# Low weight parts subtracted half a piece later, and the attention's side work in one queue

## The chip, the cores and the metric

The kernel runs on one core of a Trainium2 chip. The metric is the device time of one execution in microseconds (us). The kernel before took 1976.13 us in the median of 3 runs (1970.66 to 1978.91). Engines are called as in the profile: PE (matmul), PEld (its weight loads), DVE (VectorE), ACT (ScalarE), POOL (GpSimd), SP (the queue that issues the DMAs).

## What is computed

Two decoder layers on x (1024 tokens, 1024 features) with a memory of 256 tokens, in float32, and a final RMS norm. Layer 1 runs an RG-LRU, a dilated attention and a memory attention side by side. Layer 2 is native sparse attention (16 heads in 2 groups; compressed, selected and window branch) and a memory attention. Both add a projected, SiLU-gated result to x. The part of layer 2 around which the change moves work:

```
k_cmp = compress_tokens(kc, pe_k, phik_w1, phik_w2)
v_cmp = compress_tokens(vc, pe_v, phiv_w1, phiv_w2)
o_cmp, p_cmp = compressed_attention(q, k_cmp, v_cmp, slopes)
o_slc = selected_attention(q, ks, vs, p_cmp, slopes)
o_win, _ = banded_attention(q, kw, vw, slopes, WIN_SIZE - 1, 1)
o = gates[..., 0:1] * o_cmp + gates[..., 1:2] * o_slc + gates[..., 2:3] * o_win
...
return x + (y.astype(x.dtype) @ w_out)
```

## The kernel before

**Weights.** All projections multiply a weight matrix in pieces of 128 columns by up to eight 128-row blocks. Each piece comes by one DMA into a tile `raw` (line 201). POOL rounds it to a short float, `wh` (line 215; for the very first pieces DVE rounds a part), and DVE subtracts, `wl = raw - wh` (line 216). A product is then three matmuls: high weight by high input, high by low, low by high. `w()` (line 187) hands out piece i and at that moment asks for the load of piece i+2 and for both parts of piece i+1. `raw`, `wh` and `wl` share a ring of six buffers, so the rounding of piece i+1 must wait until PE is done with piece i-1.

**Order.** The program is written as Python generators that are advanced step by step; the steps' order is the order in which instructions are written. A scheduler then places them on each engine by what it takes to be ready, and each engine works its own list strictly in order. So an instruction at the head of a list that waits holds everything behind it.

**The start.** Eight rows of x (`xraw`, index k) arrive one by one. ACT makes the high part `xh` (line 296), DVE the low part `xl` (line 297), and PE multiplies each by the first two pieces at once. POOL adds the squares (`ssum`, line 323). At k = 6 the third and fourth piece are prefetched, and a manual dependency keeps what DVE does of that behind that k's `xl` (lines 939 to 945).

**The attention of layer 2.** `nsa_attention` (line 1609) runs 128 works: 16 iterations `it` of (half of the tokens, head group, query block), each with 8 works of two heads. A work has scores (`nsa_scores`: PE line 1507 into banks `s` or `big`, DVE line 1516 for mask and maximum into `P`, ACT line 1518 for the exponential, DVE line 1521 and POOL line 1524 to scale `P`) and their use (`nsa_apply`: PE transposes, line 1537; ACT and DVE split the result into `ph` and `pl`, lines 1541 and 1542; `nsa_av` multiplies by the values, line 1563, and ends in `ot`, line 1570). Scores run some works ahead. Between them stand two fillers: `fill` (projections of the second half of the tokens, line 239 with output `f`, drained by DVE in `st`, line 1786 or 1767; later the output projection, line 1130) and `side`.

**Side work.** `side_steps(it)` prepares what comes next: the query operands of iteration it+1 (`nsa_query`, mostly POOL), the compressed branch of iteration it+2 (`nsa_cmp`), and at some iterations the keys of the next segment (`nsa_group`). Each half of a work takes one step, in iterations 2, 6 and 11 two; what is left at the end of an iteration is run at once. `nsa_cmp` is a chain: PE scores (line 1400), DVE subtract and maximum (1403, 1406), POOL subtract (1408), ACT exponential (1410), DVE sum and reciprocal (1412, 1413), DVE gate factors `cmx` (1433), POOL multiply `ce` (1434; in the second half 1418 and 1431), then `CMPW` extra pauses, then PE transposes (1441), which ACT and DVE copy to `pc` (1442, 1443). The first matmul of an output tile (line 1558) reads `pc`.

Of the kernel before, what the change touches and what calls it, by code (L numbers as in the profile page):

```python
# [13 lines left out]
ALU = mybir.AluOpType  # L14
# [26 lines left out]
LOOK = (3, 3, 2, 3)  # L41
DELAY = 3
FILL0, FILL1 = (4, 3, 2.2, 1.8), (3.2,)
CMPW = 2


def f32(ap):
    return ap.bitcast(F32)


class Trunk:
    def __init__(self, ctx, tc, a):
        self.ctx, self.tc, self.nc, self.a = ctx, tc, tc.nc, a
        self.uid = 0
        self.rings = {}
        nc = tc.nc
        self.const = ctx.enter_context(tc.tile_pool(name="const", bufs=1))
        self.U = ctx.enter_context(tc.tile_pool(name="U", bufs=NU))
        self.W = ctx.enter_context(tc.tile_pool(name="W", bufs=NW))
        self.H = ctx.enter_context(tc.tile_pool(name="H", bufs=NH))  # L60
        self.sm = ctx.enter_context(tc.tile_pool(name="sm", bufs=2))
        self.ps = ctx.enter_context(tc.tile_pool(name="ps", bufs=1, space=PSUM))
        self.wide = None
        self.psum_layout(True)
        ctx.callback(lambda: self.bs.close())
        self.dr = ctx.enter_context(tc.tile_pool(name="dr", bufs=1, space=DRAM))
        self.ident = self.const.tile([128, 128], F32, name="ident")
        make_identity(nc, self.ident)
        self.vec = self.const.tile([128, V_N], F32, name="vec")
        nc.sync.dma_start(self.vec, a["vec"])  # L70
        self.ones = self.const.tile([128, 2], F32, name="ones")
        nc.vector.memset(self.ones, 1.0)
        self.memrow, self.memops, self.xt = None, {}, []
        self.plan, self.raws, self.split_w = [], [], []
        self.pos = 0
        self.side = []
        self.back, self.ticks = None, 0
        self.chained = None
# [105 lines left out]
    def pieces(self, *srcs, tile=None):  # L184
        self.plan += [(src, tile or self.wt) for src in srcs]

    def w(self):

        i = self.pos
        self.pos += 1  # L190
        self.prefetch(i + 3, i + 2)
        r = self.split_w[i]
        self.split_w[i] = None
        return r

    def prefetch(self, n_raw, n_split):
        nc = self.nc
        for j in range(len(self.raws), min(n_raw, len(self.plan))):
            src = self.plan[j][0]
            raw = self.wt("raw", F32, src.shape)  # L200
            nc.sync.dma_start(raw, src)
            self.raws.append(raw)
        for j in range(len(self.split_w), min(n_split, len(self.plan))):
            raw = self.raws[j]
            tile = self.plan[j][1]
            kn, c = raw.shape[1:]
            if kn * c <= 512:
                t = tile("wp", F32R, (128, 2, kn, c))
                h, l = t[:, 0], t[:, 1]
            else:  # L210
                h = tile("wh", F32R, raw.shape)
                l = tile("wl", F32R, raw.shape)
            for k0, k1 in ((0, 1), (1, kn)) if j < 2 else ((0, kn),):
                e = nc.vector if j < 2 and k0 == 0 else nc.gpsimd
                e.tensor_scalar(h[:, k0:k1], raw[:, k0:k1], 1.0, 0.0, op0=ALU.mult, op1=ALU.add)  # L215
                nc.vector.tensor_tensor(l[:, k0:k1], raw[:, k0:k1], f32(h[:, k0:k1]), op=ALU.subtract)  # L216
            self.split_w.append((h, l))
            self.raws[j] = None

    def round_to(self, h, src):  # L220
        self.nc.gpsimd.tensor_scalar(h, src, 1.0, 0.0, op0=ALU.mult, op1=ALU.add)

    def proj(self, x, halves=(0, 1)):

        w = self.w()
        ps = self.big()
        for k in range(8):
            self.proj_step(ps, w, x, k, halves)
            if x[k][0][0].shape[-1] == 512 or k % 4 == 3:
                self.tick()  # L230
        return ps

    def proj_step(self, ps, w, x, k, halves=(0, 1)):
        h, l = w
        for i, (w, p) in enumerate(((h, 0), (h, 1), (l, 0))):
            for j, t in enumerate(halves):
                v = x[k][t][p]
                o = ps[j] if isinstance(ps, list) else ps[:, 512 * j:512 * j + v.shape[-1]]
                self.nc.tensor.matmul(o, w[:, k, :], v,  # L239
                                      start=(k == 0 and i == 0), stop=(k == 7 and i == 2))  # L240
# [842 lines left out]
    def out_half(self, res):  # L1083

        nc = self.nc
        ssum = self.u("ssum", F32, (128, 512))
        for c in range(8):
            if c % 2 == 0:
                pair = self.u("x3", F32, (128, 2, 512))
            r = pair[:, c % 2, :]  # L1090
            nc.sync.dma_start(r, res[128 * c:128 * c + 128, 0:512])
            ps = self.fbank()
            for j, k in enumerate(NSA_K):
                y = self.split_pair(0, k // 2)
                if j % 4 == 0:
                    w = self.w()
                self.out_step(ps, w, y, j, slice(0, 512))
                yield
            nc.vector.tensor_tensor(r, ps, r, op=ALU.add)
            self.add_square(r, c, ssum)  # L1100
            if c % 2:
                nc.sync.dma_start(self.x3d[c - 1:c + 1].rearrange("c p n -> p c n"), pair)
            yield
# [22 lines left out]
    def out_step(self, ps, w, y, j, cols):  # L1126
        h, l = w
        yh, yl = y
        for i, (ww, v) in enumerate(((h, yh), (h, yl), (l, yh))):
            self.nc.tensor.matmul(ps[:, cols], ww[:, j % 4, :], v[:, NSA_K[j] % 2, cols],  # L1130
                                  start=(j == 0 and i == 0), stop=(j == 9 and i == 2), skip_group_check=True)
# [260 lines left out]
    def nsa_cmp(self, it):  # L1392

        nc = self.nc
# [37 lines left out]
        else:  # L1432
            nc.vector.tensor_tensor(mx[:, 3], mx[:, 2], gt[:, 0], op=ALU.mult)
            nc.gpsimd.tensor_tensor(e, e, mx[:, 3, :, None].to_broadcast([128, 8, 64]), op=ALU.mult)
        for _ in range(1 + CMPW):
            yield
        pcs = self.u("pc", F32R, (128, 2, 512))
        for quad in range(2):
# [170 lines left out]
    def nsa_attention(self, fill0, fill1):  # L1609
# [33 lines left out]
        while nxt < LOOK[0]:  # L1643
            run(self.nsa_scores(works[nxt]))
            nxt += 1
        side = iter(())
        fill, due, rate = fill0, 0.0, FILL0
        for i, W in enumerate(works):
            it = i // 8
            if i == 126:  # L1650
                self.split_pair(1, 2)
            if i % 8 == 0:
                run(side)
                side = side_steps(it)
            if i == 64:
                run(fill)
                for p in range(2):
# [2 lines left out]
            new = []  # L1660
            while nxt < min(i + LOOK[it // 4] + 1, len(works)):
                while works[nxt]["key"][0] not in self.AB:
                    next(side)
                new.append(self.nsa_scores(works[nxt]))
                nxt += 1
            ap = self.nsa_apply(W)
            n = (self.key_range(W)[1] + 1) // 2
            for h in range(2):
# [3 lines left out]
                run(fill, int(due))  # L1672
                due -= int(due)
                run(ap, (n * (h + 1)) // 2 - (n * h) // 2)
                run(side, 2 if it in (2, 6, 11) else 1)
            for sc in new:
                run(sc)
            run(ap)
# [94 lines left out]
    def fill_proj(self, x, row):  # L1773

        nc = self.nc
        for c in list(range(8)) + [16, 17] + list(range(8, 16)):
            w = self.w()
            ps = self.fbank()
            for k in range(8):
                self.proj_step(ps, w, x, k, (1,))  # L1780
# [189 lines left out]
```

## Time and profile before

| | |
|---|---|
| median of 3 runs | 1976.13 us |
| the profiled execution, its own time | 1968.65 us |
| its span from first to last instruction | 1966.9 us |
| PE busy | 1882.4 us, 96% of the span |
| DVE busy | 1181.5 us, 60% |
| ACT busy | 839.8 us, 43% |
| POOL busy | 826.0 us, 42% |
| matmuls | 10018 |
| mean granted clock of PE | 0.991 of full speed |

The profile says which engine did what and when, and for an engine that sat idle what ended the idle time. PE is nearly always busy, so only its idle stretches, and the stretches in which its clock is at half, can be won or added to. A row of the order of time begins with start and length in us, and ends with the idle time just ahead of it in brackets.

### The profile page before, as it was taken

What the parts mean: (1) busy time and instruction counts of PE and PEld (TensorE: products, weight loads), DVE (VectorE), ACT (ScalarE), POOL (GpSimd) and SP (SyncE); (2) the same over time, 40 slices, a digit from 0 to 9 for tenths busy, and PEclk for the clock granted to TensorE, in tenths of its full rate; (3) what the DMA queues carried; (4) which work ended last, traced back from release to release, by engine and by line L of the source; (5) the groups of instructions that cost most, each with busy time, mean ns of one, the idle gap of its engine ahead of it and who ended that gap; (6) DMA issues with size and microseconds to landing.
All of it is one profiled execution on the core that took longest, in us unless ns stands there. A gap on an engine that the chain in (4) does not pass through costs nothing. (4 is left out here: it accounts for less than half of the span.)

```text
span 1966.9 us, 27378 instructions
## 1 busy us (share of the span) xinstructions
PE 1882.4 (96%) x10018; PEld 1590.3 (81%) x10018; DVE 1181.5 (60%) x2293; ACT 839.8 (43%) x1780; POOL 826.0 (42%) x941
## 2 busy tenths in 40 slices
PE   8999999999999999999999999999998999988997
PEld 6789988887877777888888878787777887877886
DVE  6544336535344856562143574678688877889864
ACT  4210024423212623330034351467558666788851
POOL 6231102122124434422224433577676555567533
PEclk9999999999999999999999999999999999999999
DMA  5123311113110111132222413221221112210013
GB/s 184 54 97 122 115 53 33 33 54 107 54 47 29 43 43 43 42 121 81 83 81 91 135 62 105 78 83 63 72 93 55 52 49 80 89 57 33 12 59 98
DMA packets 57286, 141.90 MB, mean 72 GB/s; under 512 B 8256, under 2 KB 16960, under 8 KB 57152
## 3 DMA queue, kind: packets, MB, share of 16 engines
q1 hardware_dynamic: 57152, 140.16, 22.2%
q8 instruction: 79, 1.29, 0.3%
q14 instruction: 55, 0.45, 0.1%
HBM read 120.21 MB, written 19.92 MB: 71 GB/s over the span
## 5 line engine op out<-in xcount | busy, mean ns | idle before, releaser
L215 POOL TENSOR_SCALAR wh<-raw 128x1024 fp32r<-128x1024 f32 (+2 forms) x149 | 169.5, 1139 | 642.1 <-PE big L239 271.6
L216 DVE TENSOR_TENSOR wl<-raw,wh 128x1024 fp32r<-128x1024 f32 (+4 forms) x151 | 194.5, 1292 | 180.7 <-POOL wh L215 158.9
L1524 POOL TENSOR_SCALAR P<-P,nden,gates 128x640 f32<-128x640 f32 (+7 forms) x256 | 214.0, 846 | 133.7 <-DVE nden L1521 112.1
L239 PE MATMUL big<-xh,wh 128*128 128x512 f32 x752 | 258.3, 423 | 1.6 <-ACT xh L296 1.1
L239 PE MATMUL big<-xl,wh 128*128 128x512 f32 x752 | 243.2, 399 | 2.8 <-DVE xl L297 2.8
L239 PE MATMUL big<-xh,wl 128*128 128x512 f32 x752 | 235.1, 393 | 0.0
L1518 ACT ACTIVATE P<-P,nden 128x640 f32<-128x640 f32 (+7 forms) x256 | 187.6, 733 | 89.6 <-DVE nden L1516 83.9
L1542 DVE TENSOR_TENSOR pl<-t,ph 128x512 fp32r<-128x512 f32 (+1 forms) x304 | 183.3, 615 | 36.1 <-ACT ph L1541 30.8
L1541 ACT ACTIVATE ph<-t 128x512 fp32r<-128x512 f32 (+1 forms) x304 | 159.6, 534 | 57.0 <-PE t L1537 46.7
L1537 PE MATMUL t<-ident,P 128*128 128x128 f32 x1056 | 167.3, 277 | 16.8 <-DVE pl L1542 13.6
L239 PEld LDWEIGHTS big<-xl,wh 128*128 128x128 f32 x752 | 141.4, 189 | 33.6 <-DVE xl L297 3.8
L1537 PEld LDWEIGHTS t<-ident,P 128*128 128x128 f32 x1056 | 126.0, 141 | 50.7 <-DVE pl L1542 12.2
L239 PEld LDWEIGHTS big<-xh,wl 128*128 128x128 f32 x752 | 141.9, 189 | 30.1
L239 PEld LDWEIGHTS big<-xh,wh 128*128 128x128 f32 x752 | 135.2, 190 | 37.3 <-issue 15.5
L239 PE MATMUL big<-x,wh 128*128 128x512 f32 x480 | 144.3, 395 | 0.0
L1563 PE MATMUL acc<-ph,nv 128*128 128x256 f32 x528 | 128.1, 310 | 6.2 <-ACT ph L1541 5.6
L1563 PE MATMUL acc<-pl,nv 128*128 128x256 f32 x528 | 121.8, 298 | 0.0
L1516 DVE CUSTOM_DVE_ANT_0 P<-big,mask 128x640 f32<-128x640 f32 (+3 forms) x128 | 116.7, 914 | 3.6 <-PE big L1507 2.0
L239 PEld LDWEIGHTS big<-x,wh 128*128 128x128 f32 x480 | 87.8, 188 | 16.4
L1563 PEld LDWEIGHTS acc<-ph,nv 128*128 128x128 f32 x528 | 86.3, 190 | 14.1 <-ACT ph L1541 11.7
L519 DVE SCALAR_TENSOR_TENSOR df<-big,row 128x1024 f32<-128x1024 f32 x23 | 39.9, 1737 | 92.8 <-PE big L239 88.1
L239 PE MATMUL f<-x,wh 128*128 128x512 f32 x288 | 93.5, 402 | 0.0
(341 smaller groups left out, 4189.3 us busy)
## 6 DMA issues: line engine op xcount, KB each, us to landing
raw<-nw_f SPq DMA_DIRECT2D x42, 512.0 KB, 3.5
raw<-hw_dv SPq DMA_DIRECT2D x24, 512.0 KB, 3.5
raw<-hw_dil SPq DMA_DIRECT2D x22, 512.0 KB, 3.5
raw<-now SPq DMA_DIRECT2D x32, 256.0 KB, 2.6
raw<-hw_z SPq DMA_DIRECT2D x14, 512.0 KB, 3.5
raw<-how SPq DMA_DIRECT2D x16, 448.0 KB, 3.4
raw<-hw_xa SPq DMA_DIRECT2D x8, 512.0 KB, 3.5
res<-xT SPq DMA_DIRECT2D x8, 512.0 KB, 5.0
```

The lines of the kernel that those rows point to most:

```text
L215: e.tensor_scalar(h[:, k0:k1], raw[:, k0:k1], 1.0, 0.0, op0=ALU.mult, op1=ALU.add)
L216: nc.vector.tensor_tensor(l[:, k0:k1], raw[:, k0:k1], f32(h[:, k0:k1]), op=ALU.subtract)
L239: self.nc.tensor.matmul(o, w[:, k, :], v, start=(k == 0 and i == 0), stop=(k == 7 and i == 2))
L519: self.nc.vector.scalar_tensor_tensor(ot[:, sl], p.rearrange("p (i r) -> p i r", r=dil), sc, rt[:, sl], op0=ALU.mult, op1=ALU.mult)
L1516: nc.vector.tensor_tensor_reduce(ev, sv, mv, scale=1.0, scalar=3e38, op0=ALU.add, op1=ALU.min, accum_out=den[:, 0, h:h + 1])
L1518: nc.scalar.activation(e, e, AF.Exp, bias=den[:, 0, h:h + 1], scale=-1.0, accum_out=den[:, 1, h:h + 1])
L1524: nc.gpsimd.tensor_scalar(es[h], es[h], den[:, 2, h:h + 1], gt[:, 2 - br, hh:hh + 1], op0=ALU.mult, op1=ALU.mult)
L1537: nc.tensor.transpose(t[:, 256 * i + 128 * h:256 * i + 128 * h + 128], W["e"][h][:, 128 * k:128 * k + 128], self.ident)
L1541: nc.scalar.activation(ph[:, :w], t[:, :w], AF.Copy)
L1542: nc.vector.tensor_tensor(pl[:, :w], t[:, :w], f32(ph[:, :w]), op=ALU.subtract)
L1563: nc.tensor.matmul(o, V[:, k0 + k, :], x[:, 256 * i:256 * i + 256], start=False, stop=(br == 1 and k == nb - 1 and x is pl), skip_group_ch ...
```

## The change

The low part of a piece is no longer written right behind the rounding. It goes on a list, `lows`, which `weight_low()` empties: at the latest at the next `w()`, in projections and the output projection in the middle of the current piece, elsewhere at once as before. For the first two pieces nothing changes. The side generators go into one queue, which is advanced at a rate that a table `SIDE` gives for each iteration; nothing is run at once at an iteration's end, and what a work needs (`AB`, `pc`) is forced just ahead of it. The compressed branch of the first half waits four pauses, not two, before its transposes.

```
-CMPW = 2
+CMPW = (4, 2)
+SIDE = (1, 1, 1.6, 1.1, 1, 1, 1.6, 1.1, 1, 1, 1, 1.7, 1.1, 1.2, 1, 1)
...
-    def w(self):
+    def w(self, later=False):
         i = self.pos
         self.pos += 1
+        self.weight_low()
         self.prefetch(i + 3, i + 2)
+        if not later:
+            self.weight_low()
...
                 e.tensor_scalar(h[:, k0:k1], raw[:, k0:k1], 1.0, 0.0, op0=ALU.mult, op1=ALU.add)
-                nc.vector.tensor_tensor(l[:, k0:k1], raw[:, k0:k1], f32(h[:, k0:k1]), op=ALU.subtract)
+                self.lows.append((l[:, k0:k1], raw[:, k0:k1], f32(h[:, k0:k1])))
+                if j < 2:
+                    self.weight_low()
...
+    def weight_low(self):
+        while self.lows:
+            l, raw, h = self.lows.pop(0)
+            self.nc.vector.tensor_tensor(l, raw, h, op=ALU.subtract)
...
     def proj_step(self, ps, w, x, k, halves=(0, 1)):
         h, l = w
+        if k == 4:
+            self.weight_low()
...
     def out_step(self, ps, w, y, j, cols):
         h, l = w
         yh, yl = y
+        if j % 4 == 2 or j == 9:
+            self.weight_low()
...
-        for _ in range(1 + CMPW):
+        for _ in range(1 + CMPW[half]):
             yield
...
             if i % 8 == 0:
-                run(side)
-                side = side_steps(it)
+                sides.append(side_steps(it))
...
                 while works[nxt]["key"][0] not in self.AB:
-                    next(side)
+                    step()
...
+            while it not in self.pc:
+                step()
             ap = self.nsa_apply(W)
...
-                run(side, 2 if it in (2, 6, 11) else 1)
+                lag += SIDE[it]
+                for _ in range(int(lag)):
+                    step()
+                lag -= int(lag)
```

`proj`, `fill_proj` and `out_half` call `w(True)`.

DVE at the start, from the low part of the second x row on; before:

```order
L297 SCALAR_TENSOR_TENSOR xl_143<-xraw_91,vec,xh_142 128x1024
L216 TENSOR_TENSOR wl_116<-raw_93,wh_115 128x896
L297 SCALAR_TENSOR_TENSOR xl_167<-xraw_127,vec,xh_166 128x1024
L297 SCALAR_TENSOR_TENSOR xl_191<-xraw_146,vec,xh_190 128x1024
L297 SCALAR_TENSOR_TENSOR xl_215<-xraw_170,vec,xh_214 128x1024
L297 SCALAR_TENSOR_TENSOR xl_239<-xraw_194,vec,xh_238 128x1024
L297 SCALAR_TENSOR_TENSOR xl_263<-xraw_218,vec,xh_262 128x1024
L216 TENSOR_TENSOR wl_271<-raw_266,wh_270 128x1024
L297 SCALAR_TENSOR_TENSOR xl_293<-xraw_242,vec,xh_292 128x1024
```

The same place in the changed kernel (its lines 311 and 230 are 297 and 216 before):

```order
L311 SCALAR_TENSOR_TENSOR xl_143<-xraw_91,vec,xh_142 128x1024
L230 TENSOR_TENSOR wl_116<-raw_93,wh_115 128x896
L311 SCALAR_TENSOR_TENSOR xl_167<-xraw_127,vec,xh_166 128x1024
L230 TENSOR_TENSOR wl_271<-raw_266,wh_270 128x1024
L311 SCALAR_TENSOR_TENSOR xl_191<-xraw_146,vec,xh_190 128x1024
L311 SCALAR_TENSOR_TENSOR xl_215<-xraw_170,vec,xh_214 128x1024
L311 SCALAR_TENSOR_TENSOR xl_239<-xraw_194,vec,xh_238 128x1024
L311 SCALAR_TENSOR_TENSOR xl_263<-xraw_218,vec,xh_262 128x1024
L311 SCALAR_TENSOR_TENSOR xl_292<-xraw_242,vec,xh_291 128x1024
```

The low part of the third piece is written outside the stretch that the manual dependency covers and moves ahead of four `xl`. Nothing moves on POOL and ACT there. On SP the load of the last x row falls behind the load `raw_316`, which waits for a buffer that this low part frees; the changed kernel:

```order
L932 DMA xraw_194<-xT 128x1024
L932 DMA xraw_218<-xT 128x1024
L205 DMA raw_316<-hw_dil 128x1024
L932 DMA xraw_242<-xT 128x1024
L205 DMA raw_413<-hw_dil 128x1024
```

Before, `xraw_242` stands right behind `xraw_218`.

DVE in iteration 3 of the attention, from the compressed branch's sum (`cmx<-ce`) to its gate factors (`cmx<-cmx,gates`); before:

```order
L1412 TENSOR_REDUCE cmx_10453<-ce_10451 128x8
L1516 ISA P_10505,nden_10504<-s_10537,mask_7914 128x512
L1516 ISA nden_10504 128x1
L1771 SCALAR_TENSOR_TENSOR st_10511<-th_10513,st_10511 128x512
L1542 TENSOR_TENSOR pl_10526<-t_10520,ph_10525 128x512
L1413 RECIPROCAL cmx_10453<-cmx_10453 128x8
L216 TENSOR_TENSOR wl_10545<-raw_10271,wh_10544 128x1024
L1433 TENSOR_TENSOR cmx_10453<-cmx_10453,gates 128x8
```

The same in the changed kernel (1428, 1449 and 1532 are 1412, 1433 and 1516 before):

```order
L1428 TENSOR_REDUCE cmx_10432<-ce_10430 128x8
L1558 TENSOR_TENSOR pl_10494<-t_10488,ph_10493 128x512
L1429 RECIPROCAL cmx_10432<-cmx_10432 128x8
L1537 RECIPROCAL nden_10459<-nden_10459 128x2
L1532 ISA P_10509,nden_10508<-s_10510,mask_7914 128x512
L1532 ISA nden_10508 128x1
L1449 TENSOR_TENSOR cmx_10432<-cmx_10432,gates 128x8
L1794 SCALAR_TENSOR_TENSOR st_10515<-f_10276,row_7051 128x512
L1532 ISA P_10509,nden_10508<-s_10537,mask_7914 128x512
L1532 ISA nden_10508 128x1
L230 TENSOR_TENSOR wl_10545<-raw_10271,wh_10544 128x1024
```

The gate factors go ahead of the low part, and less stands between them and the sum; iteration 2 shows the same. On PE the transposes that read `ce` move behind the first four value matmuls of iteration 4.

DVE at the first low part that is subtracted behind scores of the attention; before:

```order
L1542 TENSOR_TENSOR pl_9209<-t_9205,ph_9208 128x256
L1516 ISA P_9217,nden_9216<-s_9218,mask_7914 128x128
L1516 ISA nden_9216 128x1
L1786 SCALAR_TENSOR_TENSOR st_9223<-f_9146,row_7051 128x512
L216 TENSOR_TENSOR wl_9229<-raw_9140,wh_9228 128x1024
L1516 ISA P_9217,nden_9216<-s_9237,mask_7914 128x128
L1516 ISA nden_9216 128x1
```

The same in the changed kernel (its 1558, 1532 and 1813 are 1542, 1516 and 1786 before):

```order
L1558 TENSOR_TENSOR pl_9209<-t_9205,ph_9208 128x256
L1532 ISA P_9217,nden_9216<-s_9218,mask_7914 128x128
L1532 ISA nden_9216 128x1
L1813 SCALAR_TENSOR_TENSOR st_9223<-f_9145,row_7051 128x512
L1532 ISA P_9217,nden_9216<-s_9236,mask_7914 128x128
L1532 ISA nden_9216 128x1
L230 TENSOR_TENSOR wl_9229<-raw_9140,wh_9228 128x1024
```

One score tile of `P` goes ahead of the low part. At the other low parts of the first half the place moves by none to two such tiles; POOL's list there, with the query operands ahead of `wh`, stays nearly as it was. From iteration 8 to 10 no engine's list changes, and in layer 1 only a few places do.

## Rows read from the trace of the kernel before

**Rows 1.** Stretches of the span: length, busy us (count) of PE, PEld, DVE, ACT, POOL; clock, DMA share, GB/s.
```profile
0.00:50.00 50.00, 44.13 (x184) 35.09 (x185) 31.84 (x49) 22.86 (x32) 31.66 (x27) 0.93 0.51 181
...
600.00:1050.00 450.00, 449.53 (x1966) 361.73 (x1965) 227.45 (x184) 147.25 (x167) 140.50 (x83) 1.00 0.20 65
...
1240.00:1510.00 270.00, 247.23 (x1476) 207.38 (x1474) 208.93 (x564) 168.04 (x439) 187.12 (x228) 0.99 0.24 77
1510.00:1700.00 190.00, 175.85 (x1112) 152.52 (x1112) 155.38 (x333) 125.82 (x247) 108.51 (x119) 0.98 0.19 58
1700.00:1900.00 200.00, 185.18 (x1304) 164.72 (x1303) 176.59 (x388) 166.10 (x332) 122.79 (x125) 0.99 0.11 37
```

**Rows 2.** PE, clock, DMA share, GB/s: a half-clock stretch, one at full, another at half.
```profile
15.30:18.70 3.40, 3.40 (x10) 0.50 1.04 406
...
1399.00:1409.00 10.00, 7.28 (x39) 1.00 0.29 80
1431.90:1435.30 3.40, 3.40 (x12) 0.51 0.55 217
```

**Rows 3.** Low parts that DVE waited for, and PE behind them, in order of time.
```profile
1265.80 1.23 DVE L216 TENSOR_TENSOR wl<-raw,wh 128x1024 fp32r<-128x1024 f32 x1 [3.20 <-POOL wh L215]
...
1267.29 0.33 PE L1507 MATMUL s<-K,A 128*128 128x128 f32 x1 [1.13 <-DVE nden L1516]
...
1398.33 1.23 DVE L216 TENSOR_TENSOR wl<-raw,wh 128x1024 fp32r<-128x1024 f32 x1 [3.74 <-POOL wh L215]
...
1402.02 0.47 PE L1558 MATMUL acc<-pc,vc 128*128 128x512 f32 x1 [2.39 <-DVE ot L1570]
...
1431.29 0.39 PE L1507 MATMUL s<-K,A 128*128 128x256 f32 x1 [1.80 <-DVE nden L1516]
```

**Rows 4.** Waits of PE, 1240 to 1510 us: what waited, for whom; us, times, longest.
```profile
PE s L1507 <- DVE nden L1516: 7.4, 10, 1.8
PE t L1441 <- POOL ce L1434: 4.0, 2, 2.1
PE acc L1558 <- DVE ot L1570: 3.6, 4, 2.4
...
PE t L1441 <- POOL ce L1431: 1.3, 1, 1.3
```

**Rows 5.** Waits of DVE, 1240 to 1510 us.
```profile
DVE wl L216 <- POOL wh L215: 17.4, 11, 3.7
```

**Rows 6.** The start in order of time: DVE, POOL, PE, SP.
```profile
16.62 11.00 DVE L297 SCALAR_TENSOR_TENSOR xl<-xraw,vec,xh 128x1024 fp32r<-128x1024 f32 x5
27.55 2.31 DVE L216 TENSOR_TENSOR wl<-raw,wh 128x1024 fp32r<-128x1024 f32 x1
...
20.06 2.02 POOL L215 TENSOR_SCALAR wh<-raw 128x1024 fp32r<-128x1024 f32 x1
...
39.39 1.06 POOL L215 TENSOR_SCALAR wh<-raw 128x1024 fp32r<-128x1024 f32 x1
...
14.66 0.74 PE L239 MATMUL big<-xl,wh 128*128 128x512 f32 x2 [2.30 <-DVE xl L297]
...
21.86 0.61 PE L239 MATMUL big<-xl,wh 128*128 128x512 f32 x2
...
11.28 1.61 SPq L918 DMA_DIRECT2D xraw<-xT  x2
29.89 0.33 SPq L201 DMA_DIRECT2D raw<-hw_dil  x1
```

**Rows 7.** Groups of PE's matmuls, 21 to 40 us, by shape: busy us, mean ns, idle.
```profile
L239 PE MATMUL big<-xl,wh 128*128 128x512 f32 x21 | 6.5, 389 | 0.0
```

**Rows 8.** Waits of PE, 0 to 50 us.
```profile
PE t L245 <- POOL ssum L323: 0.5, 2, 0.4
```

**Rows 9.** The two waits for `ce` in order of time: PE, DVE, POOL.
```profile
1333.77 0.63 PE L1441 MATMUL t<-ident,ce 128*64 128x128 f32 x4 [1.94 <-POOL ce L1434]
1375.33 0.63 PE L1441 MATMUL t<-ident,ce 128*64 128x128 f32 x4 [2.06 <-POOL ce L1434]
...
1372.24 1.83 DVE L216 TENSOR_TENSOR wl<-raw,wh 128x1024 fp32r<-128x1024 f32 x1
1374.00 0.15 DVE L1433 TENSOR_TENSOR cmx<-cmx,gates 128x8 f32<-128x8 f32 x1
...
1374.23 1.04 POOL L1434 TENSOR_TENSOR ce<-ce,cmx 128x512 f32<-128x512 f32 x1 [1.24 <-DVE cmx L1433]
```

More of the change, by code (lines that the diff above doesn't have):

```diff
@@ L73, in __init__ @@
         self.memrow, self.memops, self.xt = None, {}, []
-        self.plan, self.raws, self.split_w = [], [], []
+        self.plan, self.raws, self.split_w, self.lows = [], [], [], []
         self.pos = 0
@@ L223, in proj @@
     def proj(self, x, halves=(0, 1)):
-        w = self.w()
+        w = self.w(True)
         ps = self.big()
@@ L1095, in out_half @@
                 if j % 4 == 0:
-                    w = self.w()
+                    w = self.w(True)
                 self.out_step(ps, w, y, j, slice(0, 512))
@@ L1645, in nsa_attention, with step @@
             nxt += 1
-        side = iter(())
+        sides, lag = [], 0.0
+        def step():
+            while sides:
+                try:
+                    return next(sides[0])
+                except StopIteration:
+                    sides.pop(0)
         fill, due, rate = fill0, 0.0, FILL0
@@ L1776, in fill_proj @@
         for c in list(range(8)) + [16, 17] + list(range(8, 16)):
-            w = self.w()
+            w = self.w(True)
             ps = self.fbank()
```

## The prediction

> **What bounds the kernel now.** I read the stretches first. PE is busy 449.53 of 450 us between 600 and 1050, and about 92% of the attention: 247.23 of 270, 175.85 of 190 and 185.18 of 200 us [rows 1]. So PE sets the time nearly everywhere. What can be won is its idle time, which is 5.9 us in the first 50 and 22.8, 14.2 and 14.8 us in the three stretches of the attention, and the stretches in which its clock is at half. The layer-1 projections hold little. The clock is read next: matmuls run at 1.2 instead of 2.4 GHz in a stretch of 3.40 us at the start and of 3.40 at 1432, while after a wait of 2.39 us at 1399.6 it stays at 1.00 [rows 2, 3]. Such a stretch of 3.4 us loses half of it, 1.7.
>
> Then I read the waits. In 1240 to 1510, where the change moves most, PE waits 7.4 us for DVE before scores, 4.0 in two waits for `ce`, 3.6 for DVE's `ot`, 1.3 for another `ce` [rows 4]. DVE itself waits 17.4 us in 11 low parts for POOL's rounding [rows 5]; that is what the change is about. What counts is how much of these 17.4 us PE feels. The low parts in order of time say: the one at 1265.80 had waited 3.20 us, and PE behind it 1.13; the one at 1398.33 had waited 3.74, and PE 2.39; PE's wait of 1.80 at 1431.29 has another such low part ahead of it [rows 3]. Outside the attention PE does not feel it: between 600 and 1050 it is idle for 0.47 us in all [rows 1]. Low parts that come later there are worth nothing and, since the list is emptied in the middle of the piece, half a piece ahead of their first reader, cost nothing either. If that cover were gone, each piece would cost at most its low part, 1.23 us.
>
> **The start: a cost.** The changed order puts the low part of the third piece ahead of four `xl`. The five `xl` run from 16.62, 11.00 us together, 2.2 each, so the first ends at 18.8 [rows 6]. The low part now stands next, and must wait for POOL's rounding, which ran 20.06 to 22.08. Its 2.02 us beside DVE's work compare with 1.06 for the same operation at 39.39 [rows 6]; with DVE waiting it ends between 21.1 and 22.1. Then the low part takes between 1.23 us, as at 1265.80 [rows 3], and 2.31, as at 27.55 [rows 6], and the `xl` of the fourth row 2.2: ready between 24.55 and 26.6. PE began that row's `xl` products at 21.86 [rows 6], so it idles 2.7 to 4.7 us. I take 3.2: the rounding at its fast end, as DVE does nothing beside it, and the low part halfway. The next rows of x are covered again, since one `xl` of 2.2 us is followed by seven matmuls of 0.389 us [rows 7], 2.7 us of PE. A wait of 2.30 us at 14.66 stood ahead of the half-clock stretch from 15.30 [rows 2, 6]; a new one of over 2.7 us there, with PE's work still broken, is likely to bring another, 1.7 us; the wait of 2.39 without a fall [rows 2, 3] bounds this at nothing. The `ssum` waits of 0.5 us [rows 8] come later than the new gap and vanish in it. Start: 3.2 + 1.7 - 0.5 = +4.4, between +2.2 and +7.6 (4.7 and two stretches of 1.7, less 0.5).
>
> The Trainium skill, "SBUF — State Buffer", section "Who interferes with whom", says that a DVE instruction with two inputs from SBUF and a GpSimd instruction that reads SBUF lock each other out. The trace agrees where it shows 2.02 beside 1.06 for one rounding and 2.31 beside 1.23 for one low part [rows 3, 6]. By that rule a waiting DVE would leave both at their fast end, and the start would come to 2.7 + 1.7 - 0.5 = +3.9 rather than +4.4.
>
> On SP the load of the last row of x falls behind `raw_316`. That load went out at 29.89, when the low part of the third piece had set its buffer free, whereas the pairs of x rows went out from 11.28 [rows 6]. In the changed kernel that low part ends some 5 to 6 us earlier, at 22.4 to 24.4, and the last row follows. From issue to use it needs its transfer, ACT's high part and an `xl`; four rows of 2.7 us and the new gap of 3.2 put that use 14 us after 21.86, so I take nothing for it. If the transfer is slow the last row costs PE up to an estimated 1.6 us, which goes into the bound.
>
> **The two waits for `ce`: a gain.** At 1375.33 PE had waited 2.06 us for `ce`. POOL had waited 1.24 for DVE's `cmx`, which stood behind a low part of 1.83 us at 1372.24 [rows 9]. In the changed order the gate factors go ahead of that low part, so `ce` comes about 1.8 us earlier, and the transposes of this iteration move behind four value matmuls: the wait goes. The wait of 1.94 at 1333.77 [rows 9] has the same build. The distance on PE between the chain's start and its transposes is about the same there, but the gate factors come earlier. Both gone: -4.0. The bounds are none, if POOL's own list is what ends last, and all. I take all, since the trace names DVE as what POOL waited for. What is late next is DVE's score work, which PE waits for in 10 places already [rows 4].
>
> **One low part behind a score tile: a gain.** At 1265.80 DVE had waited 3.20 us with a score tile queued behind the low part, and PE behind that waited 1.13 [rows 3]. One tile now goes ahead: -1.1, bounds 0 and -1.1. At the other low parts of 1240 to 1510 the rounding stays behind the same operations in POOL's list, and the low part moves by no more than two tiles. I leave the 2.39 and the 1.80 [rows 3] where they are.
>
> **The side queue.** In iteration 6 the rate falls from 2 to 1.6 per half work and the distance from `ce` to its transposes on PE becomes shorter by about 1.5 us by my estimate. There PE waited 1.3 us for `ce` of line 1431 [rows 4]. It could grow by as much, or shrink as POOL and DVE have less at once. I take 0, and 1.3 each way. Iterations 8 to 10 are unchanged. In 11 to 14 little moves; the idle 14.8 us of 1700 to 1900 [rows 1] are taken as they are, give or take 1.
>
> **Sum.** Start +4.4, `ce` -4.0, score tile -1.1: -0.7 us. The profiled execution took 1968.65 us, so 1967.95, a ratio of 0.9996. The median of the runs shown is 1976.13, 0.4% above this execution; the ratio on it gives 1975.4. A measurement of this kernel tells about 0.5% from no change, 9.9 us: faster is below 1966.2, slower above 1986.0.
>
> **Rivals.** *A: the attention loses its DVE waits.* If the later low parts and the steady pace keep DVE from standing in front of POOL at all, then the waits for `nden` (7.4) and `ot` (3.6) [rows 4] and the half-clock stretch at 1432 (1.7) [rows 2] go too: -0.7 - 12.7 = -13.4 on the profiled execution, 1962.7 on the median. For it: 17.4 us of DVE waiting [rows 5] against some 11 us of PE's waits. Against it: the low parts stay right behind the rounding's neighbours at 1398 and 1428, with POOL's list unchanged, and half of the stretch's idle time has no low part ahead.
>
> The Trainium skill, "TensorE: Matmul & The Clock Gate", section "HAM oscillation — how this bites in real kernels", says that idle gaps between groups of matmuls send the clock down, and that each such fall is paid for anew. The rows agree at 14.66 and 1431.29 and not at 1399.6, where 2.39 us of waiting left the clock at full [rows 2, 3, 6]. If each long gap counted, A would be worth more, and the start's new gap would surely cost its 1.7.
>
> *B: the low part at the head of DVE's list at the start costs its upper bound.* Rounding and low part both run at their slow ends (4.7 us of idle), two half-clock stretches follow (3.4) and the last row of x is late (1.6): +9.2 after the 0.5. Against the gains of 5.1 that is +4.1, or 1980.2; if the `ce` waits stay too, because POOL's multiply and not DVE's gate factors ends last, it is +8.1, 1984.3; with iteration 6's wait grown by 1.3 and another half-clock stretch of 1.7 behind it, +11.1, 1987.3. It is slower than before from the point at which the start costs more than 5.1 us. For it: the slow ends are what the start shows, with POOL's squares beside DVE's low part. Against it: DVE would be idle while POOL rounds.
>
> *C: the change does not do what it says.* The scheduler may put the low part right behind the rounding's end as before, since it orders by readiness; the third order above moves it by one tile only. Then the start's cost stands alone: +4.4, 1980.5.
>
> **How the numbers follow.** My forecast has 0.56. A has 0.22, as DVE waits for 17.4 us and a steadier queue may take more of this than I can follow. B has 0.14, of which about 0.08 lies above 0.5%, since its end does and the price of a broken start may be larger than the rows of before show; C has 0.08, with 0.02 above. Faster by over 0.5%: A and 0.01 of the forecast, 0.23. Slower: 0.10. Same: 0.67. The range goes from 1962, which takes in the better half of A's results, to 1987, near the end of B.
>
> **What would show it.** A wait of PE for an `xl` near 21.9 us, 3 us long, and a half-clock stretch behind it, would show the start's cost; no such wait would show it wrong. The rows `t <- ce` of line 1434 should be gone from PE's waits in 1240 to 1510. DVE's wait for `wh` there should stay above 10 us, and the waits of PE near 1400 and 1430 should stay; if `s <- nden` falls well below 5 us and `ot` vanishes, A is right. If the last row's `xl` ends a wait of PE near 36 us, B's late load is real. PE's idle time in 600 to 1050 should stay below 1 us; if it grows to several, the low parts come too late for their readers, and the forecast fails on that step.

## The result and the profile after

The changed kernel took 1984.43 us in the median of 9 runs, the kernel before 1973.92 in 9 runs beside them: a ratio of 1.0054, 95% interval 1.0043 to 1.0066. It is slower by about 10.5 us. The forecast was 1975.4 and no change that can be measured; the time lies inside the stated range, near its upper end.

The profiled execution of the changed kernel has a span of 1981.2 us, 14.3 more than the one before. The stretches, with the columns of [rows 1]:

```profile
0.00:50.00 50.00, 41.47 (x157) 32.53 (x158) 30.80 (x46) 20.38 (x28) 31.26 (x26) 0.93 0.49 178
600.00:1050.00 450.00, 449.53 (x1975) 362.00 (x1974) 225.14 (x182) 144.68 (x165) 144.60 (x92) 1.00 0.19 63
1240.00:1510.00 270.00, 245.13 (x1412) 207.50 (x1411) 199.81 (x547) 161.11 (x421) 180.19 (x220) 0.96 0.23 73
1510.00:1700.00 190.00, 174.96 (x1123) 152.45 (x1122) 156.97 (x341) 124.03 (x250) 107.78 (x121) 0.98 0.19 58
1700.00:1900.00 200.00, 183.47 (x1278) 162.39 (x1277) 175.84 (x391) 168.49 (x334) 127.18 (x129) 1.00 0.13 44
```

Against [rows 1] PE does the same 449.53 us of work in 600 to 1050, loses 2.7 us of busy time in the first 50, and in 1240 to 1510 it is busy 245.13 rather than 247.23 us at a clock of 0.96 rather than 0.99; 1412 matmuls fall into that stretch against 1476.

A busy share does not tell where the time was lost, since the same work lies at other times in the two traces. So I matched matmuls: the n-th matmul of one line and width in the one trace with the n-th of that line in the other, and took the median of the difference of their start times in each stretch. This is how far the changed kernel lags:

| time in the kernel before, us | lag, us | what lies between |
|---|---|---|
| 100 to 1100 | 4.8 to 4.9 | the start |
| 1200 to 1236 | 4.1 | |
| 1288 to 1292 | 2.4 | a gain of 1.7 |
| 1296 to 1300 | 8.9 | a loss of 6.5, of which 2.6 come back by 1308 |
| 1460 to 1464 | 7.9 | 1.6 more since 1308 |
| 1472 to 1476 | 12.9 | a loss of 5.0 |
| 1600 to 1700 | 12.0 | |
| 1830 to 1900 | 14.6 | a loss of 2.5 |

The waits of PE in 1240 to 1510 us: what waited, for whom, us in total, times, longest. They answer to [rows 4]; lines 1523, 1574, 1457, 1447 and 1450 are 1507, 1558, 1441, 1431 and 1434 before.

```profile
PE s L1523 <- DVE nden L1532: 12.5, 12, 3.6
PE acc L1574 <- DVE ot L1586: 3.8, 3, 2.4
PE t L1457 <- POOL ce L1447: 3.2, 1, 3.2
...
PE t L1457 <- POOL ce L1450: 0.2, 1, 0.2
```

The waits for `ce` of the first half (4.0 us in [rows 4]) are down to 0.2. But the waits for DVE's scores went from 7.4 to 12.5, and the wait for the other `ce` from 1.3 to 3.2. DVE's own wait for the rounding grew from 17.4 [rows 5] to 21.0 us:

```profile
DVE wl L230 <- POOL wh L219: 21.0, 11, 4.0
```

**The place near 1294 us.** The kernel before, in order of time, DVE, POOL and then PE:

```profile
1289.36 0.42 DVE L1516 CUSTOM_DVE_ANT_0 P<-s,mask 128x256 f32<-128x256 f32 x1
...
1290.90 0.41 DVE L1516 CUSTOM_DVE_ANT_0 P<-s,mask 128x256 f32<-128x256 f32 x1
...
1293.30 1.23 DVE L216 TENSOR_TENSOR wl<-raw,wh 128x1024 fp32r<-128x1024 f32 x1 [1.97 <-POOL wh L215]
...
1292.22 1.05 POOL L215 TENSOR_SCALAR wh<-raw 128x1024 fp32r<-128x1024 f32 x1
...
1291.45 0.28 PE L1507 MATMUL s<-K,A 128*128 128x256 f32 x1
```

The changed kernel, DVE, POOL and PE:

```profile
1291.52 0.17 DVE L1537 RECIPROCAL nden<-nden 128x2 f32<-128x2 f32 x1 [1.62 <-ACT P L1534]
1295.67 1.23 DVE L230 TENSOR_TENSOR wl<-raw,wh 128x1024 fp32r<-128x1024 f32 x1 [3.99 <-POOL wh L219]
...
1297.42 0.41 DVE L1532 CUSTOM_DVE_ANT_0 P<-s,mask 128x256 f32<-128x256 f32 x1
...
1291.18 1.28 POOL L1479 TENSOR_TENSOR B<-q,A 64x512 fp32r<-64x512 f32 x1
1292.54 0.62 POOL L233 TENSOR_SCALAR A<-A 64x512 fp32r<-64x512 f32 x1
1293.23 1.27 POOL L1479 TENSOR_TENSOR B<-q,A 64x512 fp32r<-64x512 f32 x1
1294.59 1.05 POOL L219 TENSOR_SCALAR wh<-raw 128x1024 fp32r<-128x1024 f32 x1
...
1297.89 0.58 PE L1523 MATMUL s<-K,A 128*128 128x256 f32 x1 [3.64 <-DVE nden L1532]
```

Before, two score tiles `P` ran on DVE while POOL worked through the query operands, and PE had its scores' bank free in time. In the changed kernel the low part stands ahead of these two tiles. DVE waits 3.99 us for `wh`, which stands behind three query operands on POOL, and PE waits 3.64 us behind it. `wh` itself is no later than before: 1294.59 against 1292.22 us, which is the lag of 2.4. Half-clock stretches stand at this wait, at one near 1439 and at one near 1479 (length, PE busy, clock, DMA share, GB/s); the first and the last begin while PE still waits:

```profile
1297.00:1303.80 6.80, 5.91 (x19) 0.50 0.33 117
1440.30:1443.70 3.40, 3.40 (x12) 0.50 0.38 149
1477.90:1484.70 6.80, 5.22 (x20) 0.50 0.13 55
```

Between 1240 and 1900 us half clock takes 27.2 us in all in this execution, 13.6 in the one before. PE is busy in 24.1 and 12.3 us of it, and half of that is lost: 5.9 us of matmul time more than before. The wait near 1439:

```profile
1438.96 0.39 PE L1523 MATMUL s<-K,A 128*128 128x256 f32 x1 [3.08 <-DVE nden L1532]
```

### The profile page after: what moved, and what is told of

Same layout as the page of the kernel before. It is cut to its first block, busy times and chain, and to the rows that moved or that the text cites. A ratio compares the mean times of both kernels' runs of the same rounds, so it can differ in the third digit from the quotient of the medians.

```text
span 1981.2 us, 27387 instructions
## 1 busy us (share of the span) xinstructions
PE 1890.0 (95%) x10018; PEld 1599.1 (81%) x10018; DVE 1179.6 (60%) x2293; ACT 841.4 (42%) x1780; POOL 825.0 (42%) x941
## 5 line engine op out<-in xcount | busy, mean ns | idle before, releaser
L1553 PEld LDWEIGHTS t<-ident,P 128*128 128x128 f32 x1056 | 127.6, 142 | 50.0 <-DVE pl L1558 10.6
L253 PEld LDWEIGHTS big<-x,wh 128*128 128x128 f32 x480 | 87.7, 188 | 16.6 <-POOL wh L219 0.4
```

Of the source, the lines that this page charges most:

```text
L253: self.nc.tensor.matmul(o, w[:, k, :], v, start=(k == 0 and i == 0), stop=(k == 7 and i == 2))
L1553: nc.tensor.transpose(t[:, 256 * i + 128 * h:256 * i + 128 * h + 128], W["e"][h][:, 128 * k:128 * k + 128], self.ident)
```

## The experiments

All ratios are against runs of the kernel before on the same chip, with 95% intervals, from 6 to 12 runs of each kernel and 9 to 24 of the one before. A difference of two ratios is known to some 0.0015, 3 us, no better.

| kernel | ratio | interval |
|---|---|---|
| changed kernel | 1.0054 | 1.0043 to 1.0066 |
| e1_start: its start put right | 1.0031 | 1.0019 to 1.0042 |
| e2_lows: before + later low parts | 1.0024 | 1.0012 to 1.0035 |
| e3_side: changed without later low parts | 1.0034 | 1.0020 to 1.0047 |
| e5_cmpw: before + four pauses | 0.9996 | 0.9987 to 1.0005 |
| e6_rate: e1_start, all old rates | 0.9994 | 0.9985 to 1.0002 |
| e10_rate6: e1_start, old rates in 6 and 7 | 1.0020 | 1.0011 to 1.0030 |
| e12_rate2: e1_start, old rates in 11 to 13 | 1.0015 | 1.0003 to 1.0026 |
| e4_act: before, ACT rounds in the attention's first half | 0.9939 | 0.9927 to 0.9951 |
| e9_dummy: the same, POOL rounds too, for nothing | 0.9990 | 0.9982 to 0.9999 |
| e8_act_cmpw: e4_act + four pauses | 0.9936 | 0.9923 to 0.9948 |
| e7_act_after: e1_start + ACT rounds | 0.9936 | 0.9922 to 0.9950 |
| e11_act_rate: e6_rate + ACT rounds | 0.9927 | 0.9913 to 0.9942 |

**The start put right.**

```diff
                 self.prefetch(4, 3)
+                self.weight_low()
```

> The changed kernel, but the low part of the third weight piece is again subtracted inside the stretch that the manual dependency covers, so that it stands behind the xl of k = 6. Theory 1 (the start's low part is one of three separate losses): the wait of PE for an xl near 26 us goes, the matmuls of 50 to 1050 us come 4.8 us earlier, and the losses in the attention stay: about 1979.6 us, 1.003 of before. Rival (the attention's losses hang on where the start put things, or give the time back): the time stays within 2 us of the changed kernel's 1984.4, or falls by 8 or more.

It took 1978.89 us. The difference to the changed kernel, 0.0023 of 1973, is 4.5 us, give or take some 3: the start's share. PE's waits in the attention stayed, 3.63 us at 1292.99 and 3.14 at 1477.05 in this trace, so they do not hang on the start.

**The later low parts alone.**

```diff
-CMPW = (4, 2)
+CMPW = (2, 2)
...
-                sides.append(side_steps(it))
+                run(side)
+                side = side_steps(it)
...
-                lag += SIDE[it]
-                for _ in range(int(lag)):
-                    step()
-                lag -= int(lag)
+                run(side, 2 if it in (2, 6, 11) else 1)
```

> The kernel before with the later low parts alone (side steps, pauses and rates as before). Theory 1 (in the attention the low parts' own rule costs next to nothing; what moved them ahead of score tiles is the side work): only the start's 4.8 us, with 0 to 1 us back in 1240 to 1290: about 1978 to 1979 us, ratio 1.0022 to 1.0026, and no wait of PE above 2.5 us near 1294. Rival (later low parts cost the attention): start and some 9 us in the attention, ratio about 1.007.

1.0024, which is 4.7 us (2.4 to 6.9), the start's share once more. No wait above 1 us stands near 1294. In the attention the later low parts cost and win nothing in sum that can be measured. In the trace they do move waits, both ways. PE's wait of 1.13 us at 1267.29 [rows 3] is gone. The one near 1431 grew from 1.80 [rows 3] to 3.00, as the low part now stands ahead of one more score tile there; it is 3.0 to 3.1 in every kernel here that has the later low parts and POOL's rounding, and 1.1 to 1.2 in e3_side and e5_cmpw. And a wait for a load of the query is new, since that load now stands behind one more weight piece's on SP; the changed kernel does not have it.

```profile
1430.65 0.39 PE L1523 MATMUL s<-K,A 128*128 128x256 f32 x1 [3.00 <-DVE nden L1532]
...
1461.32 1.13 PE L1416 MATMUL t<-kcbd,q 128*128 128x128 f32 x8 [2.17 <-DMA q<-qd]
```

**The side work alone**, the low parts at once as before.

```diff
-                if j < 2:
-                    self.weight_low()
+                self.weight_low()
```

> The changed kernel with the low parts subtracted at once, as before: the side queue with its rates and the four pauses alone. Theory (the start costs about 4.7 us, the side work about 6, the later low parts of the attention nothing): as the changed kernel with the start put right, ratio 1.0031, with PE's waits of 3.6 near 1291, 3 near 1435 and 3.1 near 1477. Rival (the low parts and the queue cost only together): ratio 1.001 or less.

1.0034, about the 1.0031 of e1_start, from which this kernel differs by the later low parts alone: they are worth nothing that can be measured in the changed kernel either. The two parts add up, and the second loss, some 6 us, is the side work's. PE waits 3.36 us at 1293.84 here with the low part subtracted at once: the side work moved it, not the rule for low parts.

```profile
1293.84 0.58 PE L1522 MATMUL s<-K,A 128*128 128x256 f32 x1 [3.36 <-DVE nden L1531]
```

**Four pauses alone.**

```diff
-CMPW = 2
+CMPW = (4, 2)
...
-        for _ in range(1 + CMPW):
+        for _ in range(1 + CMPW[half]):
```

> The kernel before with four pauses instead of two ahead of the compressed transposes of the first half, and nothing else. Theory 1 (the pauses win the two ce waits, 4.0 us, but put the low part near 1294 us ahead of two score tiles): the ce waits of line 1434 go, a wait of PE of about 3.6 us with half clock behind it comes near 1294, and the sum is 0 to +3 us, ratio 1.000 to 1.0015. Rival (the queue and its rates did that, the pauses only win): no wait above 1.5 us near 1294 and -4 us, ratio 0.998.

0.9996, no difference. PE's waits of this kernel, in order of time:

```profile
1296.98 0.58 PE L1507 MATMUL s<-K,A 128*128 128x256 f32 x1 [3.36 <-DVE nden L1516]
...
1338.19 0.63 PE L1441 MATMUL t<-ident,ce 128*64 128x128 f32 x4 [1.93 <-POOL ce L1434]
```

The pauses alone put the low part ahead of the two score tiles: a change to the compressed branch's transposes moved an instruction that has nothing to do with them. One of the two waits for `ce` stays, 1.93 us, and the sum is nil. I had expected both to go; the other half of that gain comes from the rates: the wait is 1.9 in e6_rate too, and 0.2 where iterations 2 and 3 have the table's rates.

**The rates.** All old, then those of iterations 6 and 7 alone, then those of 11 to 13 alone, each on e1_start:

```diff
-SIDE = (1, 1, 1.6, 1.1, 1, 1, 1.6, 1.1, 1, 1, 1, 1.7, 1.1, 1.2, 1, 1)
+SIDE = (1, 1, 2, 1, 1, 1, 2, 1, 1, 1, 1, 2, 1, 1, 1, 1)
+SIDE = (1, 1, 1.6, 1.1, 1, 1, 2, 1, 1, 1, 1, 1.7, 1.1, 1.2, 1, 1)
+SIDE = (1, 1, 1.6, 1.1, 1, 1, 1.6, 1.1, 1, 1, 1, 2, 1, 1, 1, 1)
```

> The changed kernel with the start put right, and the side queue at the rates of before (2 in iterations 2, 6 and 11, else 1). Theory (the lower rate of iteration 6 brings the key gain forward less and ce late): the wait of 3.1 us for ce near 1477 and the half-clock stretch of 6.8 behind it go, the 3.6 near 1291 stays, since pauses and not rates made it: 3 to 5 us less than with the table's rates, ratio about 1.001. Rival (the queue itself, without the run at an iteration's end, is what costs): ratio stays at 1.003.

> The changed kernel with the start put right and the old rates in iterations 6 and 7 alone (2 and 1 instead of 1.6 and 1.1). Theory (iteration 6's late ce, with the half-clock stretch behind it, is most of what the table costs): the wait near 1477 falls from 3.1 to 1.3 us, the losses of 1700 to 1850 stay: 4 to 5 us less than with the table, ratio 1.0007 to 1.0012. Rival (iterations 10 to 13 cost the most): ratio 1.002 or more.

> The changed kernel with the start put right and the old rates in iterations 11 to 13 alone (2, 1, 1 instead of 1.7, 1.1, 1.2). Theory (the table costs in two places, iteration 6 and the last quarter of the attention): the 2 to 3 us that PE falls behind between 1700 and 1850 us go, the ce wait of 3.1 us near 1477 stays: ratio 1.0015 to 1.002. Rival (what the profile shows after 1700 is chance of that execution): ratio stays at 1.003.

The old rates take all of it back: 1.0031 to 0.9994, 7.3 us, give or take some 3. Those of 6 and 7 give 0.0011 of it (2.2 us), those of 11 to 13 give 0.0016 (3.2 us). Taken one by one these two are no larger than what the intervals leave open, and so is the rest, 0.0010; I leave open whether iterations 2 and 3 hold it. The expectation for iteration 6, 4 to 5 us, was too high by the medians, though the mechanism is there.

The traces show both places. From 1460 to 1476 us the lag grows by 5.0 to 5.1 us in the changed kernel, e1_start, e3_side and e12_rate2, which have the table's rate in iteration 6, and by 0.9 to 1.0 in e5_cmpw, e6_rate and e10_rate6, which do not. Between 1700 and 1860 us PE is idle for 16.2 to 16.6 us in the changed kernel, e1_start, e3_side and e10_rate6, which have the table's rates in iterations 11 to 13, and for 12.4 to 14.4 in the kernel before, e2_lows, e5_cmpw, e6_rate and e12_rate2. The wait that grows there is PE's for ACT's `ph`, 6.5 to 7.2 us against 2.8 to 3.8; why ACT is late I have not followed. Each trace is a single execution, but they agree.

The wait for `ce` in the changed kernel, in e6_rate and in e10_rate6:

```profile
1479.48 1.06 PE L1457 MATMUL t<-ident,ce 128*64 128x128 f32 x4 [3.15 <-POOL ce L1447]
```

```profile
1471.10 1.06 PE L1458 MATMUL t<-ident,ce 128*64 128x128 f32 x8 [1.33 <-POOL ce L1448]
```

```profile
1473.96 1.06 PE L1458 MATMUL t<-ident,ce 128*64 128x128 f32 x8 [1.30 <-POOL ce L1448]
```

The chain ahead of the wait, in the changed kernel and then in e6_rate: from DVE's subtraction `ce` over the sum to POOL's last multiply.

```profile
1468.45 0.68 DVE L1419 TENSOR_TENSOR ce<-cb,t 128x512 f32<-128x512 f32 x1
...
1474.21 0.69 DVE L1428 TENSOR_REDUCE cmx<-ce 128x8 f32<-128x512 f32 x1 [2.23 <-ACT ce L1426]
...
1478.36 1.06 POOL L1447 TENSOR_TENSOR ce<-ce,gates 128x512 f32<-128x512 f32 x1
```

```profile
1461.19 0.67 DVE L1420 TENSOR_TENSOR ce<-cb,t 128x512 f32<-128x512 f32 x1
...
1466.31 0.69 DVE L1429 TENSOR_REDUCE cmx<-ce 128x8 f32<-128x512 f32 x1 [0.97 <-ACT ce L1427]
...
1469.99 1.05 POOL L1448 TENSOR_TENSOR ce<-ce,gates 128x512 f32<-128x512 f32 x1 [0.62 <-DVE nden L1538]
```

From the subtraction's start to the multiply's end it is 10.97 us at the table's rate and 9.85 at the old one; from the subtraction's start to where PE begins to wait it is 7.9 us (1476.33) and 8.6 us (1469.77). The chain became 1.1 us longer, of which 0.6 lie ahead of the sum, and the distance on PE became 0.7 us shorter. Together that is the 1.8 us.

**ACT rounds the pieces of the attention's first half.** This takes POOL out of the path of the low parts.

```diff
-                e = nc.vector if j < 2 and k0 == 0 else nc.gpsimd
-                e.tensor_scalar(h[:, k0:k1], raw[:, k0:k1], 1.0, 0.0, op0=ALU.mult, op1=ALU.add)
+                if self.by_act:
+                    nc.scalar.activation(h[:, k0:k1], raw[:, k0:k1], AF.Copy)
+                else:
+                    e = nc.vector if j < 2 and k0 == 0 else nc.gpsimd
+                    e.tensor_scalar(h[:, k0:k1], raw[:, k0:k1], 1.0, 0.0, op0=ALU.mult, op1=ALU.add)
```

`by_act` holds from the first work of the attention to the 64th.

> The kernel before, but in the first half of the attention ACT instead of POOL rounds the weight pieces. Theory 1 (PE's waits of 1.1, 2.4 and 1.8 us at 1267, 1402 and 1431 come from low parts that stand at the head of DVE's list while POOL still does query operands): these three go, and the half-clock stretch at 1432 with them, 5 to 7 us less, ratio about 0.997; DVE's wait for wh falls from 17.4 us to under 6. Rival (score work on DVE is what ends last there, or ACT's own list is as late): DVE waits for ACT instead or PE's waits stay, ratio 0.999 to 1.003.

0.9939, 12 us faster than the kernel before, twice what I expected. The waits of PE and of DVE in 1240 to 1510:

```profile
PE s L1511 <- DVE nden L1520: 3.3, 7, 0.8
PE t L1445 <- POOL ce L1438: 2.7, 2, 1.8
PE t L1445 <- POOL ce L1435: 2.6, 1, 2.6
...
DVE wl L220 <- ACT wh L216: 2.2, 4, 0.8
```

DVE's wait for the rounding falls from 17.4 [rows 5] to 2.2 us, PE's wait for the scores from 7.4 to 3.3, and `ot`, 3.6 us in [rows 4], is gone. So low parts that wait do cost PE. But the gain is larger than these waits.

**Whose time was it?** POOL rounds each piece as well, into a tile that nobody reads, so that its load is that of the kernel before.

```diff
                     nc.scalar.activation(h[:, k0:k1], raw[:, k0:k1], AF.Copy)
+                    d = self.u("dum", F32R, raw.shape)
+                    nc.gpsimd.tensor_scalar(d[:, k0:k1], raw[:, k0:k1], 1.0, 0.0, op0=ALU.mult, op1=ALU.add)
```

> ACT rounds the pieces of the attention's first half, and POOL rounds each of them as well, into a tile that nobody reads, so that POOL's load stays as in the kernel before. Theory (what cost was DVE waiting at a low part behind POOL's query operands, not POOL's load): most of ACT's gain stays, ratio 0.994 to 0.996, and no wait of DVE for wh above 1 us. Rival (the gain came from 17 roundings of 1 us taken off POOL, which scales P and multiplies ce): ratio 0.999 or more.

0.9990: the rival was right. DVE waits no more than 0.8 us at a time for `wh` here, and PE waits for POOL instead:

```profile
PE s L1513 <- DVE nden L1522: 5.2, 7, 1.6
PE t L1447 <- POOL ce L1440: 4.8, 2, 2.9
...
DVE wl L222 <- ACT wh L216: 2.7, 5, 0.8
```

Some 2 us of ACT's gain came from DVE no longer waiting, and some 10 from the 1.06 us a piece, 17 pieces, that POOL was relieved of. One reservation: the dummy also holds the buffer of `raw` until POOL has read it, and takes a buffer of another ring, which I did not separate.

**Together.** ACT rounds, and four pauses; ACT rounds in e1_start; ACT rounds in e6_rate.

> The kernel before with ACT rounding the pieces of the attention's first half and four pauses ahead of the compressed transposes. Theory (the pauses cost nothing once no low part waits for POOL): no wait of PE near 1291 above 1 us although the low part stands ahead of two score tiles again; the ce wait near 1371 shrinks from 1.8: ratio 0.992 to 0.994, at or below the 0.9939 of ACT's rounding alone. Rival (the pauses cost by themselves, through the later pc): 0.9955 or more.

> The changed kernel with the start put right, and ACT rounding the pieces of the attention's first half. Theory (low parts in front of score tiles cost only while POOL is late; the rates cost by themselves): PE's waits near 1291 and 1435 go, the ce wait near 1470 and the losses after 1700 stay: about 0.994 + 0.0037 = 0.9975. Rival (with POOL free, ce is never late, and the rates cost nothing): 0.994.

> The changed kernel with the start put right, the rates of before, and ACT rounding the pieces of the attention's first half. Theory (both repairs add up): the ratio of the old rates, 0.9994, less the 0.0061 of ACT's rounding: about 0.993, like the kernel before with ACT's rounding and four pauses. Rival (the later low parts give ACT's rounding time and win in addition): 0.991 or less.

0.9936, 0.9936 and 0.9927: all at the level of e4_act, with overlapping intervals. With ACT rounding the table's rates cost 0.0009 (0.9936 against 0.9927), less than the intervals can tell, and not 0.0037, so here the rival of e7_act_after was right in its time, although PE's one wait for `ce` there was longer than ever, 4.08 us at 1455.39. What the low part near 1291 stands ahead of no longer matters: none of the three has a wait of PE above 1 us there. The pauses win nothing here either (0.9936 against 0.9939). The best of them, e11_act_rate, took 1958.04 us, 14 below the kernel before and, by the ratios, some 25 below the changed one.

## Why the prediction was wrong

The forecast was +4.4 for the start, -5.1 for the two gains and 0 for the side queue's rates: -0.7. Taken apart by the experiments, the change is +4.5 for the start (changed kernel against e1_start), +7.3 for the rates (e1_start against e6_rate) and -1.2 for all the rest (e6_rate against before): 10.6. Each of the three is known to some 3 us. So the rates, which were put at nothing, cost the most, although one of the two `ce` waits goes by them, and the gains came at most in part.

- **The start: right in size, in part by luck.** Forecast +4.4, measured 4.5 (e1_start) and 4.7 (e2_lows), with intervals of 2 to 3 us each way. The trace of the changed kernel:

```profile
18.57 2.31 DVE L311 SCALAR_TENSOR_TENSOR xl<-xraw,vec,xh 128x1024 fp32r<-128x1024 f32 x1
21.83 2.30 DVE L230 TENSOR_TENSOR wl<-raw,wh 128x1024 fp32r<-128x1024 f32 x1 [0.95 <-POOL wh L219]
24.06 11.18 DVE L311 SCALAR_TENSOR_TENSOR xl<-xraw,vec,xh 128x1024 fp32r<-128x1024 f32 x5
...
19.77 2.03 POOL L219 TENSOR_SCALAR wh<-raw 128x1024 fp32r<-128x1024 f32 x1
21.77 14.62 POOL L337 TENSOR_TENSOR ssum<-ssum,sq 128x512 f32<-128x512 f32 x7
...
26.39 0.74 PE L253 MATMUL big<-xl,wh 128*128 128x512 f32 x2 [2.43 <-DVE xl L311]
```

  The wait for the `xl` is there, 2.43 us against 3.2, and it is shorter only since PE reached it some 2 us later in this execution. A half-clock stretch stands at 27.2, as forecast. The durations went to the slow ends, 2.03 and 2.30 us, where I had taken the fast end and the middle, so the `xl` was there at 26.39, near the late end of my 24.55 to 26.6: DVE's `xl` still ran until 20.9, beside the rounding, and POOL's squares ran beside the low part. What failed was my idea that each would run alone; that POOL had the squares next on its list I had put down to B only. The Trainium skill's rule in "SBUF — State Buffer", section "Who interferes with whom", that a DVE instruction with two SBUF inputs contends with a GpSimd instruction that reads SBUF, agrees with these two durations. My estimate of +3.9 by it left the squares out. The last row of x did come late, ACT waited 4.76 us for it, and no PE wait followed: hidden, as taken.
- **Layer 1: right.** PE is busy 449.53 us in 600 to 1050 in both, and the lag there is constant.
- **The two `ce` waits and the score tile: right in place, next to worthless in sum.** The waits went from 4.0 to 0.2 us, and the score's wait of 1.13 near 1267 is down to 0.5; the lag shrinks by 1.7 us up to 1288. But the change without the start and the rates, to which 3.2 of the 5.1 belong, gains 1.2 us (e6_rate), and e5_cmpw, which has the pauses, gains nothing: the same edit makes the next loss. That this loss is what ate the gain is argued from the traces and not shown; with ACT rounding, where no long wait stands near 1291, the pauses gain nothing either (e8_act_cmpw against e4_act).
- **"At the other low parts ... the low part moves by no more than two tiles. I leave the 2.39 and the 1.80": this step failed.** I took a move of up to two tiles as harmless without looking which way it went. One low part moved ahead of two of its tiles, near 1294, by the pauses (e5_cmpw). That is 3.64 us of wait with 6.8 us of half clock at it. Another moved ahead of a tile by the rule for later low parts (e2_lows), and the wait near 1431 grew from 1.80 to 3.08, while that near 1400 stayed (2.36). The order at the first low part, shown with the change, where a tile goes ahead, is a place where it went the right way.
- **"I take 0, and 1.3 each way" for iteration 6: the second step that failed.** I had worked out that the distance becomes shorter and did not charge it. The wait grew by 1.9 us, beyond the 1.3, and again half clock came with it. The rates as a whole cost 7.3 us, the largest part of what the forecast missed, and some 3 us of that lie in iterations 11 to 13, for which I had allowed 1 us because "little moves".
- **The clock** was charged in the sum only at the start. In the attention the two long new waits each came with a half-clock stretch of 6.8 us; PE was busy in 5.91 and 5.22 us of these, so 3.0 and 2.6 us were lost, nearly as much as by the waits themselves.
- **The rivals.** The time is that of B's end, but mostly not by B's mechanism: the start's two operations were slow as B has them, but the start cost what I forecast, and the `ce` waits went; of B's further terms the grown wait of iteration 6 with half clock at it came. C's time was near for the low parts alone, though not its reason: they did move, and in sum it was worth nothing. A was wrong for the changed kernel, as DVE's wait for the rounding grew; much of what A describes happened in e4_act, at 12 us.
- **Slips in the sums**, on which nothing hangs: the third low part was to end 5.5 to 7.5 us earlier by the figures given, not 5 to 6, and B's 1984.3 and 1987.3 should be 0.1 less.

## What to carry to other kernels

When a scheduler places instructions by readiness, an edit in one branch moves others across it: list every place where an instruction that is known to wait stands on a busy in-order engine, and look on which side of its neighbours it now stands, with a sign. A distance that becomes shorter in front of a wait that is already there is a cost to be charged, not an unknown around zero. And before reordering who waits for a loaded engine, try taking work off that engine: moving 1 us a piece from POOL to ACT was worth more than any order tried here.

## What the runs showed of the hardware

A long wait of PE had a price beyond its length, and not always: 3.64 us before 1297.89 and 3.15 before 1479.48 each came with 6.8 us at half clock, 3.08 before 1438.96 with 3.4, and 2.36 before 1410.25 with none. Nor is the price of one wait the same in every kernel: that near 1294, 3.4 to 3.7 us long, came with 6.8 us at half clock in the changed kernel and e1_start, and with 3.4 in e3_side, e5_cmpw, e6_rate and e12_rate2. In the eleven kernels above whose start is that of before, the lag at 50 to 100 us against the profiled execution of the kernel before lay between -0.4 and 2.9 us: a single execution does not tell a start's cost to better than that, which is why the start was judged by medians.
